# Where two small loads of weights are queued, in a combine of expert outputs that streams 100 MB

## The chip, the cores and the metric

The kernel runs on one core of a Trainium2 chip. Its engines that matter here are VectorE (in the profile DVE), ScalarE (ACT) and SyncE (SP), and the 16 DMA engines that carry data between HBM and the on-chip memory, SBUF. The metric is the time of one execution in microseconds, as the device measures it; of several runs the median counts. The names with a q (SPq, ACTq) are the queues in which an engine's sequencer issues transfers and waits for semaphores.

## The reference

```
weights = combine_weights[..., np.newaxis]
return np.sum(expert_outputs * weights, axis=2).astype(np.float32)
```

`expert_outputs` is 16 x 1024 x 2 x 512 (batch, sequence, k, hidden) and `combine_weights` 16 x 1024 x 2, both float32. For each of the 16,384 tokens the outputs of two experts, rows of 512, are each multiplied by one number and added. 67 MB are read and 33.5 MB are written.

## The kernel before

The tokens are spread over the 128 partitions, 128 for each partition. The first 120 of a partition (`main`) are a contiguous run of HBM, cut into ten tiles of J = 12 tokens; the last 8 (`LAST`) are a second run and make the eleventh tile. The helper `rows` gives, for a token's place and a count, the part of the tensor in one or the other run. A tile `et` holds 12 tokens x 1024 values for every partition, 48 KB of it, and the pool `ipool` has four such buffers. The result is written into the first half of the same buffer (`ot`), so a buffer comes free when its store has landed.

All weights of a partition, 256 numbers, lie in one tile `wt`. Two transfers bring them (L54 to L57): 120 KB for the first 120 tokens (960 bytes for a partition) and 8 KB for the last 8 (64 bytes for a partition). Both are the first instructions in ScalarE's queue. A one-element activation behind them (L60) makes ScalarE load its table early.

The loop (L62) runs over the eleven tiles. SyncE issues the loads (L69): the first tile in two pieces, the first two tokens (1,024 KB, cut into rows of 4 KB) and the other ten (5,120 KB), every other tile in one. The first four tiles need no buffer to come free; the load of tile g from 4 on waits until the store of tile g - 4 has landed. For the first nine tiles VectorE multiplies the whole tile by the weights (L78), adds the halves (L79), and ScalarE issues the store (L80). In the last two tiles ScalarE multiplies the first expert's rows, token by token (L86). VectorE does the rest, for the tenth tile as a whole (L101, L102) and for the last one token by token (L90), and SyncE issues both stores (L103). The scheduler that builds the program keeps the program's order on each engine but for small shifts: it puts the store of the ninth tile (tile 8, counted from 0) between the activations of the tenth.

Each engine issues in its own order, and an instruction that waits holds up everything behind it on that engine. SyncE has the loads and the last two stores, ScalarE the weights, the other stores and its activations. SyncE's transfers are in queue q1 and ScalarE's are in q10.

Of the kernel before, what the change touches and what calls it, by code (L numbers as in the profile page):

```python
# [1 line left out]

# [4 lines left out]


@with_exitstack
def kernel(  # L10
    ctx: ExitStack,
    tc: tile.TileContext,
    expert_outputs: bass.AP,
    combine_weights: bass.AP,
    out: bass.AP,
):

    nc = tc.nc  # L20
    b, s, k, h = expert_outputs.shape
    assert k == 2
    n = b * s
    P = nc.NUM_PARTITIONS
    per = n // P
    assert per * P == n
    J, LAST = 12, 8
    main = per - LAST
    assert main % J == 0
    eo = expert_outputs.rearrange("b s k h -> (b s) (k h)")  # L30
    cw = combine_weights.rearrange("b s k -> (b s) k")
    o = out.rearrange("b s h -> (b s) h")

    def rows(x):

        a = x[0 : P * main, :].rearrange("(p t) f -> p t f", p=P)
        b = x[P * main : n, :].rearrange("(p t) f -> p t f", p=P)
        return lambda t, c: a[:, t : t + c, :] if t < main else b[:, t - main : t - main + c, :]

    eo, cw, o = rows(eo), rows(cw), rows(o)  # L40

    dt = mybir.dt.float32
    mult = mybir.AluOpType.mult
    add = mybir.AluOpType.add
    copy = mybir.ActivationFunctionType.Copy

    last = main // J

    wpool = ctx.enter_context(tc.tile_pool(name="w", bufs=1))
    ipool = ctx.enter_context(tc.tile_pool(name="in", bufs=4))  # L50

    wt = wpool.tile([P, per * k], dt)

    for t, c in ((0, main), (main, LAST)):  # L54
        nc.scalar.dma_start(
            out=wt[:, k * t : k * (t + c)].rearrange("p (t k) -> p t k", k=k), in_=cw(t, c)
        )  # L57

    warm = wpool.tile([P, 1], dt)
    nc.scalar.activation(out=warm, in_=nc.const_aps.tensor(1.0, (P, 1), dt), func=copy)  # L60

    for g in range(last + 1):  # L62
        et = ipool.tile([P, J, k * h], dt)

        ot = et.rearrange("p j f -> p (j f)")[:, 0 : J * h].rearrange("p (j f) -> p j f", f=h)
        t0, c = g * J, J if g < last else LAST

        for a, m in ((0, 2), (2, c - 2)) if g == 0 else ((0, c),):
            nc.sync.dma_start(  # L69
                out=et[:, a : a + m],  # L70
                in_=eo(t0 + a, m),
                max_dma_last_dim=k * h * 4 if g + a == 0 else None,
            )
        if g < last - 1:

            wb = wt[:, g * J * k : (g + 1) * J * k].unsqueeze(2).to_broadcast([P, J * k, h])
            ek = et.rearrange("p j (k h) -> p (j k) h", k=k)
            nc.vector.tensor_tensor(out=ek, in0=ek, in1=wb, op=mult)  # L78
            nc.vector.tensor_tensor(out=ot, in0=et[:, :, 0:h], in1=et[:, :, h : 2 * h], op=add)  # L79
            nc.scalar.dma_start(out=o(t0, c), in_=ot)  # L80
            continue


        for i in range(c):
            t = t0 + i
            nc.scalar.activation(  # L86
                out=et[:, i, 0:h], in_=et[:, i, 0:h], func=copy, scale=wt[:, 2 * t : 2 * t + 1]
            )
            if g == last:
                nc.vector.scalar_tensor_tensor(  # L90
                    out=ot[:, i, :],
                    in0=et[:, i, h : 2 * h],
                    scalar=wt[:, 2 * t + 1 : 2 * t + 2],
                    in1=et[:, i, 0:h],
                    op0=mult,
                    op1=add,
                )
        if g < last:
            w1 = wt.rearrange("p (t k) -> p t k", k=k)[:, t0 : t0 + c, 1:2]
            x1 = et[:, :, h : 2 * h]  # L100
            nc.vector.tensor_tensor(out=x1, in0=x1, in1=w1.to_broadcast([P, c, h]), op=mult)  # L101
            nc.vector.tensor_tensor(out=ot, in0=et[:, :, 0:h], in1=x1, op=add)  # L102
        nc.sync.dma_start(out=o(t0, c), in_=ot[:, 0:c])  # L103


# [1 line left out]
_INS = ['expert_outputs', 'combine_weights']  # L107
_OUTS = [((16, 1024, 512), 'float32')]


# [23 lines left out]
```

## Time and profile before

| | |
|---|---|
| median of 7 runs | 239.09 us (238.93 to 240.9) |
| the profiled execution | 238.93 us, its span 237.2 us |
| DMA | 3728 packets, 100.80 MB, mean 425 GB/s |
| VectorE busy | 193.9 us (82%) |
| ScalarE busy | 14.0 us (6%) |
| the whole-tile multiply, L78 | 9 x 12.96 us |
| the whole-tile add, L79 | 9 x 6.56 us |
| a full tile's load, issue to landing | 29.9 us (median of 9) |
| a store from ScalarE, issue to landing | 32.9 us (median of 9) |
| the weights, issue to landing | 120 KB: 4.2 us; 8 KB: 17.0 us |

The span is the time from the first to the last instruction that the profile shows; the execution's own time is 1.7 us longer. Times of a line are of a profiled execution and are given from the span's start. The time from issue to landing contains what a transfer waits for others in its queue. The share of DMA is the mean over the 16 engines.

### The profile page before, as it was taken

The page shows a single profiled execution, that of the slowest core. Times are in us where ns is not written, and L with a number is a line of the kernel's source. Part 1 is how long each engine was busy: PE and PEld are TensorE (multiplying, and loading weights), DVE is VectorE, ACT ScalarE, POOL GpSimd, SP SyncE. Part 2 cuts the span into 40 slices and gives each one's busy share as a digit, 9 for nine tenths or more (in the row PEclk, how much of TensorE's full clock was granted, in tenths as well). Part 3 has the DMA queues.
Part 4 walks back from the last instruction along what each step waited for, and adds up shares of the span by engine and source line. Part 5 has one row for each costly group of instructions (what it writes and reads, how often), then busy time and mean ns, then how long its engine had stood idle before and what let it go on. Part 6 is the DMA issues. An engine that isn't in the chain of part 4 may idle for free.

```text
span 237.2 us, 154 instructions
## 1 busy us (share of the span) xinstructions
DVE 193.9 (82%) x28; ACT 14.0 (6%) x22; POOL 0.2 (0%) x4
## 2 busy tenths in 40 slices
DVE  0009999999999999999999889969996998785710
ACT  2000000000000000000000000000000000740800
POOL 0000000000000000000000000000000000000000
DMA  8999999979899999999797999999997979999997
GB/s 308 443 465 398 398 431 497 398 332 531 357 439 444 419 464 464 398 398 531 332 531 332 464 410 452 464 464 398 398 522 340 531 332 464 459 403 442 398 442 310
DMA packets 3728, 100.80 MB, mean 425 GB/s; under 512 B 528, under 2 KB 656, under 8 KB 912
## 3 DMA queue, kind: packets, MB, share of 16 engines
q1 hardware_dynamic: 2144, 72.35, 71.1%
q10 hardware_dynamic: 1584, 28.44, 27.9%
HBM read 67.24 MB, written 33.55 MB: 425 GB/s over the span
## 4 chain that ended last, share of the span: by engine, by line
DMA 59%; DVE 33%; ACT 2%; DVEq 0%; ACTq 0%; issue 0%; SPq 0%
DMA et<-in_expert_outputs_dram 30%; DMA out_dram<-et 29%; DVE et L78 22%; DVE et L79 11%; ACT et L86 2%; DVE et L90 1%; DVEq L129 0%; ACTq L129 0%; SPq L69 0%; DVEq L78 0%; ACTq L86 0%
## 5 line engine op out<-in xcount | busy, mean ns | idle before, releaser
L78 DVE TENSOR_TENSOR et<-et,wt 128x12288 f32<-128x12288 f32 x9 | 116.6, 12956 | 25.0 <-DMA et<-in_expert_outputs_dram 25.0
L79 DVE TENSOR_TENSOR et<-et 128x6144 f32<-128x6144 f32 x9 | 59.0, 6558 | 0.3
L86 ACT ACTIVATE et<-et,wt 128x512 f32<-128x512 f32 x20 | 12.5, 711 | 209.1 <-DMA et<-in_expert_outputs_dram 209.1
L90 DVE SCALAR_TENSOR_TENSOR et<-et,wt 128x512 f32<-128x512 f32 x8 | 5.6, 746 | 3.9 <-ACT et L86 3.7
L101 DVE TENSOR_TENSOR et<-et,wt 128x6144 f32<-128x6144 f32 x1 | 6.6, 6557 | 2.3 <-DMA et<-in_expert_outputs_dram 2.3
L102 DVE TENSOR_TENSOR et<-et 128x6144 f32<-128x6144 f32 x1 | 6.6, 6558 | 0.9 <-ACT et L86 0.9
L60 ACT ACT_TABLE_LOAD x1 | 1.3, 1283 | 1.7 <-PEq L118 1.7
L60 ACT ACTIVATE warm<-const-float32-1.0 128x1 f32<-128x1 f32 x1 | 0.2, 203 | 0.0
L118 POOL MEMSET const-bfloat16-1.0<- 128x1 bf16 x1 | 0.1, 103 | 0.0
L118 POOL MEMSET const-uint8-127<- 128x1 uint8 x1 | 0.1, 102 | 0.0
L118 POOL MEMSET const-float32-0.0<- 128x1 f32 x1 | 0.1, 100 | 0.2 <-issue 0.2
L118 POOL MEMSET const-float32-1.0<- 128x1 f32 x1 | 0.1, 99 | 0.0
## 6 DMA issues: line engine op xcount, KB each, us to landing
et<-in_expert_outputs_dram SPq DMA_DIRECT2D x9, 6144.0 KB, 29.9
out_dram<-et ACTq DMA_DIRECT2D x9, 3072.0 KB, 32.9
et<-in_expert_outputs_dram SPq DMA_DIRECT2D x1, 5120.0 KB, 17.0
et<-in_expert_outputs_dram SPq DMA_DIRECT2D x1, 4096.0 KB, 25.1
out_dram<-et SPq DMA_DIRECT2D x1, 3072.0 KB, 14.7
out_dram<-et SPq DMA_DIRECT2D x1, 2048.0 KB, 10.0
et<-in_expert_outputs_dram SPq DMA_DIRECT2D x1, 1024.0 KB, 5.1
wt<-in_combine_weights_dram ACTq DMA_DIRECT2D x1, 120.0 KB, 4.2
```

Of the source, the lines that this page charges most:

```text
L60: nc.scalar.activation(out=warm, in_=nc.const_aps.tensor(1.0, (P, 1), dt), func=copy)
L78: nc.vector.tensor_tensor(out=ek, in0=ek, in1=wb, op=mult)
L79: nc.vector.tensor_tensor(out=ot, in0=et[:, :, 0:h], in1=et[:, :, h : 2 * h], op=add)
L86: nc.scalar.activation(out=et[:, i, 0:h], in_=et[:, i, 0:h], func=copy, scale=wt[:, 2 * t : 2 * t + 1])
L90: nc.vector.scalar_tensor_tensor(out=ot[:, i, :], in0=et[:, i, h : 2 * h], scalar=wt[:, 2 * t + 1 : 2 * t + 2], in1=et[:, i, 0:h], op0=mul ...
L101: nc.vector.tensor_tensor(out=x1, in0=x1, in1=w1.to_broadcast([P, c, h]), op=mult)
L102: nc.vector.tensor_tensor(out=ot, in0=et[:, :, 0:h], in1=x1, op=add)
L118: nc = _bacc.Bacc("TRN2", target_bir_lowering=False, num_devices=1)
```

## The change

Both weight loads are issued by SyncE and not by ScalarE. The first stands behind the load of the first two tokens and ahead of the rest of tile 0; the second, for the last tile's tokens, stands behind the load of the fourth tile. The one-element activation becomes ScalarE's first instruction. The number of buffers gets a name and stays 4. The computation and the sizes of all transfers are unchanged.

```diff
-    J, LAST = 12, 8
+    J, LAST, BUFS = 12, 8, 4
...
-    ipool = ctx.enter_context(tc.tile_pool(name="in", bufs=4))
+    ipool = ctx.enter_context(tc.tile_pool(name="in", bufs=BUFS))
 
     wt = wpool.tile([P, per * k], dt)
 
-    for t, c in ((0, main), (main, LAST)):
-        nc.scalar.dma_start(
+    warm = wpool.tile([P, 1], dt)
+    nc.scalar.activation(out=warm, in_=nc.const_aps.tensor(1.0, (P, 1), dt), func=copy)
+
+    def load_weights(t, c):
+        nc.sync.dma_start(
             out=wt[:, k * t : k * (t + c)].rearrange("p (t k) -> p t k", k=k), in_=cw(t, c)
         )
-
-    warm = wpool.tile([P, 1], dt)
-    nc.scalar.activation(out=warm, in_=nc.const_aps.tensor(1.0, (P, 1), dt), func=copy)
 
     for g in range(last + 1):
...
                 max_dma_last_dim=k * h * 4 if g + a == 0 else None,
             )
+
+            if g + a == 0:
+                load_weights(0, main)
+            elif g == BUFS - 1:
+                load_weights(main, LAST)
         if g < last - 1:
```

## The prediction

> **What bounds the kernel now.** I read the DMA queues first, then the busy time by stages, then the chain that ended last, then SyncE's waits, and last the first 40 us of the timeline and the rows of the weights' tile. The page's part on DMA queues comes first, because reading 67.24 MB and writing 33.55 MB is nearly all that this kernel does:
>
> ```profile
> q1 hardware_dynamic: 2144, 72.35, 71.1%
> q10 hardware_dynamic: 1584, 28.44, 27.9%
> HBM read 67.24 MB, written 33.55 MB: 425 GB/s over the span
> ```
>
> q1 is SyncE's queue and q10 is ScalarE's. Both run on the same 16 DMA engines, and the last column is the time that their packets took as a share of all 16 over the span. 71.1% + 27.9% = 99.0% of 237.2 us is 234.8 us: the packets leave about 2.4 us of the span free. The stages show where that is (per row: length, then busy time of VectorE, ScalarE and GpSimd, the clock, the DMA share, GB/s; a packet is booked where it starts, so a share can pass 1):
>
> ```profile
> 0.00:1.60 1.60, 0.00 (x0) 0.00 (x0) 0.20 (x4) 1.00 0.00 0
> 1.60:4.00 2.40, 0.00 (x0) 1.49 (x2) 0.00 (x0) 1.00 0.91 269
> 4.00:18.40 14.40, 0.03 (x1) 0.00 (x0) 0.00 (x0) 1.00 1.07 456
> 18.40:38.00 19.60, 19.57 (x3) 0.00 (x0) 0.00 (x0) 1.00 1.02 441
> ...
> 60.00:216.00 156.00, 145.94 (x16) 7.47 (x12) 0.00 (x0) 1.00 1.00 432
> 216.00:226.40 10.40, 6.42 (x9) 5.02 (x8) 0.00 (x0) 1.00 1.01 433
> ...
> 236.00:237.20 1.20, 0.00 (x0) 0.00 (x0) 0.00 (x0) 1.00 0.00 0
> ```
>
> Nothing moves for 1.60 us at the front and 1.20 us at the back; between 1.6 and 4 us the engines start up, and from then on they have packets all the time. At 432 GB/s the 2.40 us of start-up would carry 1.04 MB, and at 269 they carried 0.65 MB, so the start-up loses 0.39 MB / 432 GB/s = 0.9 us. That is all that an edit at the front can find. VectorE, busy for 193.9 us, has 43 us of idle time and is not the bound, though the chain that ended last names it:
>
> ```profile
> DMA 59%; DVE 33%; ACT 2%; DVEq 0%; ACTq 0%; issue 0%; SPq 0%
> ```
>
> The chain goes back through VectorE for the tiles that were in SBUF already. The DMA engines are full beside it, so a microsecond saved on VectorE would only move a transfer in a queue that doesn't run dry. What SyncE does meanwhile:
>
> ```profile
> SPq L69 <- DMA out_dram<-et: 173.9, 7, 45.6
> SPq L69 <- DMA et<-in_expert_outputs_dram: 15.0, 1, 15.0
> ```
>
> After its first five loads SyncE waits for stores to land before it may refill a buffer. Its own issuing time is not scarce. The start:
>
> ```profile
> 0.72 0.97 ACTq L55 DMA_DIRECT2D wt<-in_combine_weights_dram  x2
> 0.73 2.52 SPq L69 DMA_DIRECT2D et<-in_expert_outputs_dram  x5
> 1.72 1.28 ACT L60 ACT_TABLE_LOAD   x1 [1.72 <-PEq L118]
> ...
> 18.38 12.96 DVE L78 TENSOR_TENSOR et<-et,wt 128x12288 f32<-128x12288 f32 x1 [18.38 <-DMA et<-in_expert_outputs_dram]
> ...
> 37.96 0.35 ACTq L80 DMA_DIRECT2D out_dram<-et  x1
> ```
>
> The rows of the weights' tile give their issue (ns, shortest, median and longest of the two) and the time from issue to landing:
>
> ```profile
> L55 ACTq DMA_DIRECT2D wt<-in_combine_weights_dram x2: 446/468/491, 0.7 to 1.2; - x2
> ...
> DMA to landing us min/median/max: 4.2/10.6/17.0
> ```
>
> The 8 KB transfer, issued at 1.2, landed 17.0 us later, at about 18.2. So ScalarE's queue is already empty for 20 us when the first store enters it at 37.96. What the change says it brings there is mostly there before.
>
> **The change part by part.** The sum is made against the profiled execution: 238.93 us, of which 237.2 are its span and 1.7 lie around it. The median of the runs shown is 239.09, 0.16 above it.
>
> 1. The two issues leave ScalarE (0.97 us, 0.72 to 1.69). Its table load moves up to about 0.7. ScalarE's next work for a tile is at 202.80, so this is worth 0 by itself. The first load may gain: the chain shows 0.42 us for its issue, with ScalarE issuing beside it, and later issues of the line have a median of 0.328. If that is the neighbour's doing, the first packet comes 0.09 us earlier. Bounds: 0, and a gain of 1.0 us, if the whole start-up loss of 0.9 goes too. I take a gain of 0.1, since the remaining loss is that of a first transfer with nothing before it, which stays.
>
> 2. The weights' packets. In the first 38 us q10 carried only them: 288 packets, 0.13 MB, 1.1% of the 16 engines' time, or 0.42 us. The same packets now go through q1. They are moved and not removed: 0. Between 4 and 18.4 us, where they alternated with the loads, the rate was 456 GB/s, after it 441, with no weights; so the alternation cost nothing that could come back. Bounds: 0.4 either way, their whole time.
>
> 3. The first weight issue on SyncE stands ahead of the 5,120 KB of tile 0. SyncE needs 0.33 to 0.57 us for an issue, ScalarE needed 0.49; the 5,120 KB are issued at 0.73 + 0.42 + 0.49 = 1.64 instead of 1.15. A first packet came 1.60 - 0.73 = 0.9 us after the issue's start, so theirs can come from 2.5. The queue needs them when 1,024 KB and 120 KB are through: 1.6 + 2.7 (1.17 MB at 432) + 0.9 of start-up = 5.2. Cover of 2.7 us, cost 0; bare, it would be 0.49. The first multiply, at 18.38, waits for the 5,120 KB, which lie behind the weights in the same queue: it needs no new wait. Tile 0's own loads move by less than 0.5 us in either direction, and VectorE's 43 us of idle time takes that.
>
> 4. The second weight issue on SyncE, behind tile 3's load. In the built order it waits for the semaphore of the first two tokens, which landed at 0.73 + 5.1 = 5.8; SyncE comes there at 0.73 + 2.52 + 0.49 = 3.7, so it stands for 2 us and issues for 0.45. Behind it is the load of tile 4, issued at 63.99, when the first store has landed (37.96 + 26.0). SyncE's own spare time is 58 us; q1 holds 25 MB, 58 us at 432 GB/s. Cost 0. Its 8 KB land after tile 3's load (issued near 2.9, 69.3 us to landing, so 72); they are first read for the last tile, at 219.76.
>
> 5. ScalarE's queue has its first transfer at 37.96 instead of 0.72, so a queue's first start (0.9 us by the row above) falls on the first store. q1 holds loads until 72, so the engines don't stand. Cost 0; bare, 0.9.
>
> 6. In the built order the store of tile 8 now stands behind 7 and not 8 activations of tile 9. It was issued at 203.10, during the first of them, and lands 24.8 us later, at 228, with 8 us of other stores behind it. At most one activation (0.71) earlier, worth 0.
>
> Sum: 238.93 - 0.1 = 238.8, and with the 0.16 to the median 239.0 us.
>
> A rule against the change, on parts 3 and 4. The rows first: the two issues lasted 0.49 and 0.45 us beside SyncE's five. The Trainium skill, page "DMA: Bandwidth & Descriptors", section "Issuing engines are not separate DMA queues", says that all issuing engines feed the same 16 DMA engines, so that issuing from several at once saves nothing but sequencer time. The trace agrees that the engines are shared (99.0% together). Taken alone, the rule lets this change give back the saved 0.94 us, and the time would be 240.0; by the rows, where SyncE is 2.7 and 58 us ahead, it is 239.0.
>
> **The rivals.**
>
> R1, slower: q1 runs dry at the small transfer. Between 4 and 6 us q1 is now the only queue. If the 120 KB are through before the 5,120 KB are ready, the engines stand for a new start: 0.9 from issue to packet and 0.9 of start-up, +1.8, 240.8 us. It decides from the point where the 5,120 KB come later than 5.2 us. Against it: that needs a 2.7 us delay, and the boundary of 1,024 to 5,120 KB showed none (456 GB/s). The second one, near 72 us, has stores beside it.
>
> R2, slower without a cause in the edit: four of the seven runs lie at 238.93 to 239.09, three at 239.99 to 240.9. Nothing in the profile says what lifts the three. If the changed kernel's median falls among them, it is 240.0 to 240.9, about 240.5.
>
> R3, faster: the start-up loss was two queues starting at once. All of part 1's upper bound comes: 239.09 - 1.0 = 238.1 us. For it: the weights' packets took their places among the first loads'. Against it: the loss is there before the packets can be alternating much, and 0.42 us of them have to be carried somewhere.
>
> **How the numbers follow.** The measurement can tell about 0.5%, or 1.2 us, from no change: under 237.9 is faster, over 240.3 slower. Forecast 0.68, R1 0.08, R2 0.13, R3 0.11. Slower: R1, and 0.08 of R2 (its part above 240.3): 0.16. Faster: 0.05 of R3, which ends just short of the bound, and 0.03 for the kernel before falling among its own higher runs where the two are compared: 0.08. The rest is 0.76. The range goes from R3's 238.1 to R1's 240.8.
>
> **What would show it.** Right: both queues again sum to about 99.0% of the span, q1 with some 0.2% more and q10 less; nothing moves for 1.5 to 1.6 us at the front; the rate from 4 to 18.4 us is as before; SyncE's wait for stores starts later and ends at the same time. Wrong: a stage between 4 and 8 us with a share well under 1 (R1), a first multiply over 0.5 us away from 18.38, or a start-up stage near 430 GB/s (R3). The prediction fails too if the first store, as its queue's first transfer, lowers the rate between 38 and 60 us.

## The result, and the profile after

The changed kernel takes 240.96 us in the median of 23 runs (239.15 to 243.93); the kernel before took 239.10 in 60 runs beside it (238.93 to 240.9). The ratio of the means is 1.0048 [1.0034, 1.0062]; it leaves out four slow runs, at 242.74 to 243.93 and over 1.5% above the fastest, of which nothing on record says what sets them apart, and with them it would be 1.0068. By the ratio that is half a per cent, at the edge of what the forecast called no change; the median lies beyond 240.3, from which the forecast said slower, and 0.16 us above the end of its range. The best run, 239.15, is within 0.3 us of the kernel before; but only 3 of the 23 lie within 0.5 us of it, against 32 of the 60 runs of the kernel before beside them and 100 of its 137 in the sets that follow. The upper runs are not the same either: the 28 of the kernel before lie at 239.85 to 240.9, most of the changed kernel's at 240.4 to 241.4. So it is mostly the typical run that moved.

The profiled execution of the changed kernel is 240.01 us, its span 238.2, 1.08 above the profiled execution before. A second one, taken later, is 240.11. Both lie about 0.9 us below the median: the profile shows part of the loss, and no profile of a typical run at 241 was caught.

The DMA queues of the kernel after (packets, MB, share of the 16 engines' time):

```profile
q1 hardware_dynamic: 2432, 72.48, 71.2%
q10 hardware_dynamic: 1296, 28.31, 27.6%
HBM read 67.24 MB, written 33.55 MB: 423 GB/s over the span
```

The 288 packets of the weights have gone from q10 to q1, as the prediction said. The two shares make 98.8% of 238.2 us, 235.3 us, where it was 234.8: the same bytes took 0.5 us more, and the engines stood for 2.9 us instead of 2.4. The stages of the kernel after show where (length, busy time of VectorE, ScalarE and GpSimd, clock, DMA share, GB/s):

```profile
1.60:4.00 2.40, 0.00 (x0) 0.61 (x2) 0.00 (x0) 1.00 0.85 265
4.00:18.40 14.40, 0.18 (x1) 0.00 (x0) 0.00 (x0) 1.00 1.06 456
...
38.00:60.00 22.00, 21.97 (x3) 0.00 (x0) 0.00 (x0) 1.00 0.98 411
...
76.00:84.00 8.00, 8.00 (x2) 0.00 (x0) 0.00 (x0) 1.00 1.11 443
...
226.40:234.00 7.60, 3.71 (x6) 2.19 (x4) 0.00 (x0) 1.00 0.94 403
226.40:236.00 9.60, 3.71 (x6) 2.19 (x4) 0.00 (x0) 1.00 0.97 418
236.00:237.00 1.00, 0.00 (x0) 0.00 (x0) 0.00 (x0) 1.00 0.24 98
```

and four of the same stages before (the rows from 226.40 overlap):

```profile
76.00:84.00 8.00, 8.00 (x2) 0.00 (x0) 0.00 (x0) 1.00 1.02 442
...
226.40:234.00 7.60, 0.00 (x0) 0.00 (x0) 0.00 (x0) 1.00 1.01 433
226.40:236.00 9.60, 0.00 (x0) 0.00 (x0) 0.00 (x0) 1.00 0.98 418
236.00:237.00 1.00, 0.00 (x0) 0.00 (x0) 0.00 (x0) 1.00 0.00 0
```

Up to 60 us hardly anything is lost: the start-up runs at 265 GB/s where it ran at 269, the rest is as before. Between 76 and 84 us the packets took a share of 1.11 instead of 1.02 for the same rate, (1.11 - 1.02) x 8 = 0.7 us more. The row from 226.4 to 234 has 403 GB/s instead of 433, but a packet is booked where it starts, and the next 2 us make it up: from 226.4 to 236 both kernels move 418 GB/s. In this run, then, the engines don't stand before 236; they end later.

How much later can be read from the packets. Their records don't name the engine, but packets that follow each other without a gap make sixteen chains, one for each engine. Before, all sixteen end between 235.8 and 236.0 us; here fifteen end between 236.2 and 236.7, and one at 237.1. The 0.7 us near 80 us, on all engines, and 0.4 us on this one make up the 1.08 us of this run.

What happens just before 76 us is in the queues' parts from 72.4 to 76.0 us. After:

```profile
q10 hardware_dynamic: 62, 1.52, 98.2%
q1 hardware_dynamic: 63, 0.00, 1.2%
```

Before:

```profile
q1 hardware_dynamic: 32, 1.57, 100.8%
q10 hardware_dynamic: 16, 0.39, 25.3%
```

This is the reading on which the rest hangs. The 8 KB of the last tile's weights are rows of 64 bytes, 128 packets, eight for each engine. They stand in q1 behind tile 3's load, and there they meet the second store in q10. The two queues take turns by packet, not by byte: 63 packets of 64 bytes and 62 packets of a store went through in the same 3.6 us. The store moved 1.52 MB, the loads nothing; before, the loads moved 1.57 MB there and the store 0.39. The Trainium skill, page "DMA: Bandwidth & Descriptors", section "Queues, rings and completion order", says that an engine goes round between the queues it has work for packet by packet; 62 against 63 agrees, where the profile counts each row as a packet.

So the store of tile 1 landed at 77.4 instead of 85.6, and everything behind the small packets in q1 came late. The page's DMA issues of the kernel after (x count, KB each, median us to landing):

```profile
et<-in_expert_outputs_dram SPq DMA_DIRECT2D x9, 6144.0 KB, 38.1
out_dram<-et ACTq DMA_DIRECT2D x9, 3072.0 KB, 28.1
...
out_dram<-et SPq DMA_DIRECT2D x1, 2048.0 KB, 7.3
```

with the small transfer in the list of transfers, and the timeline where VectorE and ScalarE wait for it:

```profile
wt<-in_combine_weights_dram SPq DMA_DIRECT2D x1, 8.0 KB, 71.9
```

```profile
97.72 12.96 DVE L83 TENSOR_TENSOR et<-et,wt 128x12288 f32<-128x12288 f32 x1 [1.56 <-DMA et<-in_expert_outputs_dram]
...
223.58 5.02 ACT L91 ACTIVATE et<-et,wt 128x512 f32<-128x512 f32 x8 [9.47 <-DMA et<-in_expert_outputs_dram]
```

Loads take 38.1 us from issue to landing instead of 29.9, stores 28.1 instead of 32.9. Only part of the loads' 8.2 us is delay: since store 1 lands early, tile 5's load is issued at 77.46 instead of 85.69, and the next one at 103.18 instead of 107.51. Every load from tile 4's on lands 3.8 us later than before, tile 4's at 97.7 instead of 93.9. Tile 4's multiply, which ran at 96.23 without a wait, waits for its load and starts at 97.72. The last load lands at about 223.5 instead of 219.7, the last store is issued at 230.13 instead of 226.32. Beside the last store only store 9 feeds the engines, until 232.6 (before until 231.5), so the stock of other work is 2.5 us where it was 5.2. In this run that was still enough. The chain that ended last has more of the loads now; their share of it was 30% and the stores' 29%:

```profile
DMA et<-in_expert_outputs_dram 37%; DMA out_dram<-et 23%; DVE et L83 22%; DVE et L84 11%; ACT et L91 2%; DVE et L95 1%; DVEq L134 0%; ACTq L134 0%; SPq L69 0%; SPq L58 0%; DVEq L83 0%; ACTq L91 0%
```

### The profile page after: what moved, and what is told of

The parts are those of the page before. It is cut to its first block, busy times and chain, and to the rows that moved or that the text cites. A ratio compares the mean times of both kernels' runs of the same rounds, so it can differ in the third digit from the quotient of the medians.

```text
span 238.2 us, 154 instructions
## 1 busy us (share of the span) xinstructions
DVE 194.1 (81%) x28; ACT 14.0 (6%) x22; POOL 0.2 (0%) x4
## 4 chain that ended last, share of the span: by engine, by line
DMA 60%; DVE 33%; ACT 2%; SPq 0%; DVEq 0%; issue 0%; ACTq 0%
DMA et<-in_expert_outputs_dram 37%; DMA out_dram<-et 23%; DVE et L83 22%; DVE et L84 11%; ACT et L91 2%; DVE et L95 1%; DVEq L134 0%; ACTq L134 0%; SPq L69 0%; SPq L58 0%; DVEq L83 0%; ACTq L91 0%
## 6 DMA issues: line engine op xcount, KB each, us to landing
et<-in_expert_outputs_dram SPq DMA_DIRECT2D x9, 6144.0 KB, 38.1
out_dram<-et ACTq DMA_DIRECT2D x9, 3072.0 KB, 28.1
```

## The experiments

The first theory (T) is this one: the late small packets give the store of tile 1 the loads' turns, the loads run behind from there, and the time is lost in the meeting near 80 us and at the end. Its rivals were: the place of the 120 KB on SyncE, with its slowed packets near 5 us (C); a ScalarE queue that is empty when the first store enters it (E), against a loss that comes wherever the first stores meet running loads (W); the moment at which the first store is issued (B); and chance, the upper runs that the kernel before has too. Unless said, an experiment computes the whole output. "n of m near the best" counts runs within 0.5 us of that kernel's own fastest; in the kernel before it is 73% of the runs in these sets (69 to 83% by set), so a ratio of 1.002 mostly tells how many runs lie about 1 us up.

### One part of the change at a time

The early weights as changed, the late ones back on ScalarE at the start:

```diff
-    def load_weights(t, c):
-        nc.sync.dma_start(
+    def load_weights(t, c, queue=nc.sync):
+        queue.dma_start(
...
                 load_weights(0, main)
-            elif g == BUFS - 1:
-                load_weights(main, LAST)
+                load_weights(main, LAST, nc.scalar)
```

> The 120 KB of weights stay in SyncE's queue behind the first two tokens; the 8 KB go in ScalarE's queue at the start. Theory T (the 64-byte packets of the 8 KB, behind tile 3's load, take turns with the first stores' packets, so the stores run ahead, their queue runs empty, and its restart costs the engines 0.6 us): as before, 239.1 us, one loss of 0.6 us near 41 us and none near 80. Rival Q (the first store suffers as the first transfer of ScalarE's queue): as before too. Rival S (the 120 KB ahead of the 5,120 KB cost the time): as after, 240 to 241 us.

Measured: 239.79 us (239.04 to 240.96, 12 runs), ratio 1.0021 [1.0, 1.0042], 6 of 12 near the best. The opposite, the 120 KB back on ScalarE and the 8 KB as changed:

```diff
-                load_weights(0, main)
+                load_weights(0, main, nc.scalar)
             elif g == BUFS - 1:
                 load_weights(main, LAST)
```

> The 120 KB go in ScalarE's queue at the start; the 8 KB stay in SyncE's queue behind tile 3's load. Theory T: as after, 240 to 241 us, with the 8 KB landing near 77 us, store 1 near 77 instead of 85.6, and tile 4's load some 4 us later than before. Rival Q: as before, 239.1, since ScalarE's queue has been started. Rival S: as before, 239.1.

Measured: 239.79 us (239.13 to 241.03, 12 runs), ratio 1.0026 [1.0004, 1.0048], 5 of 12. The queues behave as T says: store 1 landed at 77.3, tile 4's load at 96.8, loads took 38.1 and stores 27.7 us, as in the kernel after. But the ratio is about half of the change's, and its profiled run (239.13, among its best) shows no extra packet time near 80 us (share 1.00), and the engines don't stand at the end (433 GB/s from 226.4 to 234). In that run the order that T names cost nothing by itself; it opens the way to a loss. And the early part alone, barely resolved, costs about as much, which T can't explain; the two add up to nearly the change's 1.0048, though each interval goes down to nearly 1. The first experiment's profiled run (240.73) shows C's sign: a packet of the 5,120 KB took 0.57 us longer at 5.3 us, and the chain of packets that holds it ends at 237.8, 1.8 us after the other fifteen.

### The late weights elsewhere

Behind tile 1's load, where they come up in q1 at another time (in the second kernel `g == 2`, behind tile 2's):

```diff
-            elif g == BUFS - 1:
+            elif g == 1:
                 load_weights(main, LAST)
```

> As after, but the 8 KB stand behind tile 1's load and not tile 3's, so their packets come near 32 us, before any store is issued (37.8). Theory T: no store can gain turns, 239.1 us, the loads and stores timed as before (store 1 landing near 85.6). Rival Q and rival S: as after, 240 to 241.

> As after, but the 8 KB stand behind tile 2's load, so their packets come near 50 us, in the middle of the first store. Theory T: store 0 lands near 55 us instead of 63.9, the stores' queue is empty until store 1 is issued at 57.3, and a second loss of 0.6 us stands near 60 instead of near 80: 240 to 241 us. Rivals Q and S: as after, 240 to 241, with no sign at 60 us.

Measured: behind tile 1, 240.07 us (239.05 to 240.89, 12 runs), 1.0028 [1.0009, 1.0048], 2 of 12. Its loads and stores take 30.5 and 33.8 us, as before the change, so T's 239.1 missed: without any trading of turns the upper runs are still there. Behind tile 2, 240.50 us (239.14 to 241.19, 12 runs), 1.0031 [1.0006, 1.0057], 4 of 12. Here the small packets did meet the first store, which landed at 56.4 with the 8 KB at 56.5 (T had expected 55), loads take 37.6 us and the last one lands at 224.0; the expected second loss near 60 us wasn't there. Its last store was issued at 230.66, and the engines had nothing for about 0.4 us, in the mean, near 231.

Both loads at the front of q1, behind the 5,120 KB of tile 0, where no store can meet them:

```diff
-            if g + a == 0:
+            if g == 0 and a > 0:
                 load_weights(0, main)
-            elif g == BUFS - 1:
                 load_weights(main, LAST)
```

> As after, but both weight loads stand in SyncE's queue behind the whole of tile 0, so their packets come near 18 us, with no store about and no packet of a tile waiting behind the 4 KB rows of the first two tokens. ScalarE's queue is empty up to the first store, as in after. Theory C, if what hurts near 5.3 us belongs to the start-up: as before, 239.1 us. If it belongs to small packets ahead of large ones: slowed packets near 18.5 us and 239.8. Rival Q (the first store as the first transfer of its queue): 240 to 241.

> The eighth experiment's kernel once more, beside the two others and on the same chip. If its 1.0021 was a real difference: 1.002 again, with most runs above 239.3. If it was chance: 1.000, with two runs in three near 239.1 as in the kernel before.

Measured: 240.02 us (239.06 to 240.84, 12 runs), 1.0021 [1.0002, 1.0041], 3 of 12; and again, 239.23 us (238.97 to 240.83, 12 runs), 1.0016 [0.9993, 1.0039], 7 of 12. By the middles of the intervals more than half of the loss is gone without the meeting near 72 us, but both intervals reach into the change's own, and whether the rest is real in this kernel is not settled. C's slowed packets near 5 us are not in their profiles. They do go with the place of the 120 KB: between 5.1 and 5.7 us single packets of 40 KB took 0.16 to 0.72 us longer than their like in each of the six profiles with the 120 KB ahead of the 5,120 KB in q1, and in none of the other fourteen.

### The small packets added to the kernel before

This leaves the weights as they were before and adds small loads that nothing reads. First two of 8 KB in rows of 64 bytes, eight packets per engine each, behind tiles 3 and 5 on SyncE; then one of 8 KB in 16 rows of 512 bytes, one packet per engine, behind tile 3:

```diff
+        if g in (3, 5):
+            xt = wpool.tile([P, LAST * k], dt, name=f"extra{g}")
+            nc.sync.dma_start(out=xt.rearrange("p (t k) -> p t k", k=k), in_=cw(main, LAST))
```

```diff
+        if g == 3:
+            xt = wpool.tile([16, 128], dt, name="extra")
+            src = combine_weights.rearrange("b s k -> (b s k)")
+            nc.sync.dma_start(out=xt, in_=src[0 : 16 * 128].rearrange("(p f) -> p f", p=16))
```

> The kernel before, its weights in ScalarE's queue as they were, and two more loads of the same 8 KB (128 rows of 64 bytes, into tiles that nothing reads) in SyncE's queue, behind the loads of tiles 3 and 5. Theory C: each hands some 8 turns to the stores and sets the loads back by 3.8 us against them; the last load lands near 227 us instead of 219.7, the last store is issued near 234 instead of 226.3, and the DMA engines stand at the end: 241 to 243 us. Rival S (only the 120 KB ahead of the 5,120 KB cost): 239.1 us.

> The kernel before, and one more load of 8 KB in SyncE's queue behind tile 3's load, as 16 rows of 512 bytes, into a tile that nothing reads: the same bytes as the late weights, but one packet for each DMA engine where those have eight. Theory C (a small packet takes a whole turn from the loads, whatever its size): the loads lose one or two turns, store 1 lands near 84 us and not near 77, no second loss near 80 us; as before, 239.1. If the mere presence of a small transfer in SyncE's queue did it: as in the second experiment, 239.8, ratio 1.0026.

Measured: 241.16 us (239.31 to 242.45, 12 runs), 1.0064 [1.0033, 1.0095], 3 of 12; and 239.14 us (239.08 to 240.61, 12 runs), 0.9999 [0.9983, 1.0014], 11 of 12. The intervals are apart: 8 KB in one packet per engine cost nothing that twelve runs can tell, and two of them in eight packets per engine cost 0.3 to 1%. The pair differs in the number of loads too, though: one load in eight packets is the second experiment, and its interval, from 1.0004, overlaps that of the one packet. The queues of the second from 72.4 to 76.0 us:

```profile
q1 hardware_dynamic: 47, 0.79, 51.4%
q10 hardware_dynamic: 31, 0.76, 49.1%
```

16 of q1's 47 packets are the small ones and 31 are loads; the loads keep moving 0.79 MB. The last load lands at 221.7, so half of the change's delay of the loads is there, at no cost. The stage near 80 us differs accordingly; one small packet per engine, then two loads of eight:

```profile
76.00:84.00 8.00, 8.00 (x2) 0.00 (x0) 0.00 (x0) 1.00 1.02 442
```

```profile
76.00:84.00 8.00, 8.00 (x2) 0.00 (x0) 0.00 (x0) 1.00 1.07 443
```

The size of the delay at the end was overestimated: with two loads the last load landed at 223.0 and the last store was issued at 229.65 in the profiled run, where T had 227 and 234. Loads take 42.4 us and stores 25.6, but the second small load adds little to the first.

The times of all runs together are plainer than the pair. In five kernels a small load of eight packets per engine meets a store: the changed one, the second and fourth experiments, the two added loads, and the changed one with a later store (below). 25 of their 71 runs lie above 240.96 us. None of the other 321 does, 197 of the kernel before and 124 of the other experiments. So the meeting does lift the upper runs.

### Looking again at both kernels

The same kernels once more, for the profile of an upper run:

> The changed kernel once more, for a second trace. Theory C (two costs: single large packets are slowed near 5.3 us right behind the 120 KB in the same queue, so one or two DMA engines fall behind for the rest; and the 8 KB near 77 us give store 1 the turns of tile 4's load): slow first packets of the 5,120 KB again, the spread of one load's sixteen completions over 0.4 us and growing, the last load landing near 223 to 226 us, 240 to 241.5 us. If the cost were in one of the two alone, the sign of the other would be missing.

> The kernel before once more, for a second trace. Theory C: no slowed packet near 5.3 us, store 1 landing near 85.6 us and the last load near 219.7; 239.0 to 239.2 us, or up to 240.5 where a DMA engine falls behind for another reason, near 41 us.

> The kernel with two more loads of 8 KB behind tiles 3 and 5 once more, for a second trace, since its runs went from 239.3 to 242.4 us. Theory C: where it is slow, the sixteen completions of a load are 2 us or more apart, the last load lands near 225, and the DMA engines stand for a while before the last store.

The changed kernel gave 240.11 us. Near 80 us its share is 1.07, so the second loss is there again, while the slowed packets near 5 us, which C rests on, are small (0.16 us); its last load lands at 223.6. One engine ends at 237.2, the others by 236.4; it lost 1.0 us near 81 us. The kernel with two small loads gave 240.88; its last load landed at 223.4 and the last store was issued at 230.0, T's 225 again too late; little stands at its end.

The kernel before gave 239.85, one of its own upper runs. Two stages show it, the end and the stretch from 41.2 to 42.9 us, just after the first store comes in. Its end, and the queue in that stretch:

```profile
236.00:237.00 1.00, 0.00 (x0) 0.00 (x0) 0.00 (x0) 1.00 0.12 49
```

```profile
q10 hardware_dynamic: 3, 0.07, 10.1%
```

In the first profile of this kernel q10 has no packet in that stretch and nothing moves at the end after 236. Here three of the 16 engines took the store's first packet a turn earlier than the others, and the load's packet behind it took about 1.0 us longer on each. At the end three engines stop at 236.7 to 236.9 and the others by 236.3; that these are the same three is likely, but the records don't name them. As far as the packets show, no engine takes over work from another, and all are full, so one that falls behind at 41 us ends late. The time is that of the slowest of the 16, and a mean over them hides it.

### The front of ScalarE's queue

If the empty queue costs something at the first store (E), a queue kept filled should not. The kernel before with two more loads in rows of 64 bytes on ScalarE:

```diff
+    for p in (P, 64):
+        xt = wpool.tile([P, LAST * k], dt, name=f"extra{p}")
+        nc.scalar.dma_start(
+            out=xt[0:p].rearrange("p (t k) -> p t k", k=k), in_=cw(main, LAST)[0:p]
+        )
```

> The kernel before, and behind the weights in ScalarE's queue two more loads of 64-byte rows (128 and 64 rows, into tiles that nothing reads), so that this queue takes turns with the loads until near 43 us and the first store finds it filled: the opposite of what the change aims at. Theory E (the 0.6 us near 41 us, which every trace shows and which makes single DMA engines fall behind, is the price of a queue that starts from empty beside running loads): that loss goes, fewer runs lie near 240, 238.4 to 238.8 us. Rival W (the price is that of the first writes to HBM among reads): the loss moves with the first store to some 44 us, 239.1 to 239.5.

Measured: 240.14 us (239.28 to 240.49, 6 runs), 1.0042 [1.0025, 1.0058], 1 of 6. The queue had packets until 41.8 us, and the loss of about 0.6 us between 41 and 47 us, which the kernel before and after have too, stayed as it was. (It is summed from the packets: there they took 0.6 us per engine longer than elsewhere, where one of 48 KB takes 1.81 us and one of 24 KB 0.91 us.) E falls; W, that the loss comes where a stream of stores first meets running loads, is left, though the loss didn't move to 44 us and the time missed W's too. Yet this kernel has the whole old front, and its 192 small packets more at the start cost nearly as much as the change.

If ScalarE's queue in the first 18 us matters, giving its load back should help. The kernel with both loads behind tile 0, and on ScalarE the two loads of the kernel before, into a tile that nothing reads; then only the 8 KB of them:

```diff
+    xt = wpool.tile([P, per * k], dt, name="extra")
+    for t, c in ((0, main), (main, LAST)):
+        nc.scalar.dma_start(
+            out=xt[:, k * t : k * (t + c)].rearrange("p (t k) -> p t k", k=k), in_=cw(t, c)
+        )
```

> Both weight loads in SyncE's queue behind tile 0, as in the eighth experiment (ratio 1.0021), and the same two loads in ScalarE's queue at the start, as before, into a tile that nothing reads. If traffic in ScalarE's queue during the first 18 us is what the kernel before had ahead of the others: 239.1 us, ratio 1.000. If small loads in SyncE's queue cost: ratio 1.002 again, 239.8 to 240.

> Both weight loads in SyncE's queue behind tile 0, as in the eighth experiment, and one more load of the 8 KB in ScalarE's queue at the start, into a tile that nothing reads. If traffic in ScalarE's queue ahead of the first store keeps DMA engines from falling behind: ratio 1.000 to 1.0005 (0.1 us for the extra packets). If not: 1.002 again.

And the reverse, the 120 KB on ScalarE at the start and the 8 KB on SyncE behind tile 1:

```diff
-                load_weights(0, main)
+                load_weights(0, main, nc.scalar)
-            elif g == BUFS - 1:
+            elif g == 1:
```

> The missing corner of the table: the 120 KB in ScalarE's queue at the start, the 8 KB in SyncE's queue behind tile 1's load, where no store can take their turns. If the 0.2% of the kernels that have the 120 KB in SyncE's queue belongs to the place of the 120 KB: ratio 1.000, 239.1 us. If any small load in SyncE's queue brings it: 1.002, 239.8 to 240.

Measured: with the weights loaded twice, 239.50 us (239.43 to 240.67, 12 runs), 1.0026 [1.0012, 1.004], 8 of 12. Its best runs are 0.4 us above those of the kernel before; that is the 0.42 us of packets which are now moved twice (0.18%), and about 0.08% is left. With the 8 KB alone, 240.13 us (239.05 to 240.44, 10 runs), 1.0026 [1.0006, 1.0047], 1 of 10. The reverse, 240.10 us (239.40 to 240.48, 12 runs), 1.0034 [1.0021, 1.0047], 3 of 12. So neither the place of the 120 KB nor early small packets on ScalarE is the cause alone; of these three only the one with all of the old front's packets comes near the old distribution. The profile of the reverse (240.29 us) shows the same picture as the kernel before in its upper run, in the stretch at 41.2 to 42.9 us and at the end:

```profile
q10 hardware_dynamic: 2, 0.05, 6.7%
```

```profile
236.00:237.00 1.00, 0.00 (x0) 0.00 (x0) 0.00 (x0) 1.00 0.15 66
```

### The moment of the first store

One cause that all these edits could share is a small shift of the first store against the loads' packets (B). It can be moved alone: an addition on VectorE, which nothing reads, between the multiply and the add of tile 0. With 616 numbers the store is issued at 38.76 instead of 37.96, with 1192 at 39.72; and 616 in the kernel after:

```diff
+            if g == 0:
+                xt = wpool.tile([P, 616], dt, name="extra")
+                x = et.rearrange("p j f -> p (j f)")[:, 0:616]
+                nc.vector.tensor_tensor(out=xt, in0=x, in1=x, op=add)
```

> The kernel before, with one more VectorE operation (616 numbers a partition, about 0.80 us, result unread) between the multiply and the add of tile 0, so that the first store is issued 0.8 us later against the loads. Theory B (what counts is where the first store's issue falls against the packet boundaries of the sixteen DMA engines: boundaries come every 1.81 us; in every trace so far they fall 1.1 to 1.7 us behind the issue and the loads lose some 0.6 us; where one falls later than about 1.65, that engine takes the store a turn early and ends 1 us behind the others; where they fell 0.1 to 0.7 us behind the issue, as for the second store of the fourth experiment, hardly anything was lost): boundaries at 0.3 to 0.6, the loss near 41 us mostly gone, no run near 240: 238.5 to 239.0, ratio 0.996 to 0.998. Rival N (the upper runs have nothing to do with the issue's place): 239.1 with a third of the runs near 240, as before.

> The same with 1192 numbers, about 1.40 us, so that the next boundaries fall 1.5 to 1.85 us behind the issue, across the limit. Theory B: several engines on either side, most runs near 240 or above, ratio 1.003 to 1.006. Rival N: 239.1 with a third of the runs near 240.

> The changed kernel with the 0.80 us operation of the sixteenth experiment. Its two encounters, the first store near 41 us and the third near 80, both move to boundaries 0.3 to 0.8 us behind the issue; the late 8 KB still give store 1 the turns of tile 4's load, and the last load still lands near 223. Theory B: 238.6 to 239.3, ratio 0.997 to 1.001, so that the changed order of transfers costs nothing by itself. Theory T (the turns and the shorter stock at the end cost by themselves) and rival N: 240 to 241, ratio 1.003 to 1.005.

Measured: 239.43 us (239.05 to 239.77, 12 runs), 1.0003 [0.9988, 1.0017]; 239.56 us (239.05 to 240.1, 12 runs), 1.0011 [0.9997, 1.0025]; in the kernel after 240.54 us (239.05 to 242.77, 12 runs), 1.0042 [1.0023, 1.0062]. The first removed the runs from 239.8 up (none of 12, where the kernel before beside it had 8 of 29) but brought 6 of 12 at 239.54 to 239.77; the second was expected mostly near 240 or above and had 2 of 12 over 240. The loss at 41 us stayed in the first, about 0.7 us. So the moment shifts the distribution a little, and it isn't what makes the changed kernel slow: with the store later it is as slow as without. That run's profile (240.81 us) is the nearest to a typical one that was caught:

```profile
226.40:234.00 7.60, 4.41 (x7) 3.00 (x5) 0.00 (x0) 1.00 0.93 400
...
236.00:237.00 1.00, 0.00 (x0) 0.00 (x0) 0.00 (x0) 1.00 0.70 295
```

Its last load lands at 224.3 and its last store is issued at 230.94, 0.8 us after that of the changed kernel. Here the engines do stand: from 226.4 to 236 they move 399 GB/s instead of 418, and in the chains of packets eleven of them have nothing for 0.3 to 0.8 us near 231, 0.4 us in the mean of the sixteen. Fourteen end at 236.7 to 236.9 and two at 237.6 and 237.9, when the kernel before has nothing left to do.

## Why the prediction was wrong

**The front was right in the mean.** The start-up stage ran at 265 GB/s (269 before), so part 1's gain of 0.1 and the rival R3's 1.0 us weren't there; the first multiply began at 18.22 instead of 18.38. Part 2: 456 GB/s from 4 to 18.4 us in both. Part 3: the 5,120 KB were issued at 1.73 (1.64 predicted), and there is no gap between 4 and 8 us: R1's dry queue did not come. But single packets there took longer, which no mean shows, and the first experiment leaves the cost of this part open, at 1.0021 [1.0, 1.0042]. Part 5: 411 GB/s from 38 to 60 us in both, so the first store in an empty queue costs nothing more than it did before, and the experiment with the filled queue agrees.

**The failed step is part 4**, "Cost 0. Its 8 KB land after tile 3's load ..., so 72". SyncE did wait and issue as described, at 5.67, and its own time is indeed free. But the 8 KB landed at 77.6 and not at 72: 128 packets of 64 bytes were costed as 8 KB, and each engine's eight of them each cost a whole packet of a store in the other queue. In place of the cost of 0 stood 0.7 us near 80 us in the first profile and (1.07 - 1.02) x 8 = 0.4 in the second. The prediction looked for what the small transfer would wait for, and not for what waits behind it in q1. R1 even named the place, "The second one, near 72 us, has stores beside it", and took it as a protection: the stores do keep the engines busy, but in the turns of the loads, which the last tile needs first.

**The last store was in no part of the sum.** Part 6 looked at the store of tile 8 and rightly gave it 0: it was issued 0.28 us after the first activation of tile 9 began, as before (0.30). But since the loads land 3.8 us later, the last store is issued 3.8 us later too, with 2.5 us of other work beside it and not 5.2. In the two profiles of the changed kernel, where it was issued at 230.1 and 230.2, that covered it; in the two where it came at 230.66 and 230.94 the engines stood for about 0.4 us.

**The sum itself was made over means.** It added shares of 16 engines, and a loss on one to three of them vanishes in such a share: 0.12 in one row of 1 us in the upper run of the kernel before, with 0.92 us on the whole execution.

**The rule that was weighed** gave 240.0, nearer than the forecast, but by a cause that isn't there: SyncE's two issues delayed nothing, as the equal rate from 4 to 18.4 us and the wait until 5.67 show.

**R2 was given too little.** Its words, slower without a cause in the edit, put the chance at 0.13 and the time at 240.0 to 240.9. In fact 20 of 23 runs lie above 239.65, with the median just beyond R2's end. The share of runs near the best goes with the kernel: 73% in the kernel before (53% in the 60 runs beside the change), 92% with one small packet per engine, 8 to 58% where the weights' places were changed and nothing was loaded twice. It isn't fixed in one kernel either: two sets of the same one had 3 and 7 of 12. Still, a spread of four low and three high runs was a sign of something that an edit can move, and it was read as chance.

**What the runs show, and what stays open.** Shown: the trading of turns at 72 us and its delay to the end (profiles of both kernels, of the 120 KB put back, and of the added loads), and that such a meeting costs time, since no run above 240.96 us is without one. That one packet per engine costs nothing is measured, to within 0.14%; that the packets and not the number of loads make the difference is argued from the turns. The size isn't split cleanly: 0.0048 in all, while the edits to the front with no late small load on SyncE beside a store have ratios of 1.0016 to 1.0042, with overlapping intervals. The late load's own share of the change can thus lie anywhere from little to about 0.3%. The other part shows, in the profiles that caught it, as one to three engines that end 0.4 to 2 us after the others. In some they took a turn early at the first store; in the first, third and fourth experiments chains that end late hold the packets slowed near 5 us. The place of the 120 KB, early small packets on ScalarE, an empty queue and the moment of the store were each moved alone, and none accounts for it. Its cause stays open, and so does a typical run of 241, which no profile caught. No kernel of the study was measurably faster than the kernel before.

## What to carry to other kernels

Count a transfer's packets per engine, not its bytes, when another queue is full beside it: each small packet lets a whole large packet of the other queue pass, so small rows belong where no other queue competes, or into one packet per engine. A row of one stage can move a packet's time into the next row, so join the rows before reading that engines stand, and compare landings before calling a longer time from issue a delay. In this kernel, bound by DMA, the time was that of the slowest of the 16 engines, so look at the last stage of the profile and at the spread of runs before costing an edit at nothing. Ask of a moved transfer not only what it waits for, but what waits behind it in its new queue.

## What was unexpected of the hardware

- Two queues shared the engines packet for packet whatever their size: 62 packets with 1.52 MB against 63 with 4 KB, in 3.6 us.
- About 0.6 us is lost from 41 to 47 us, where the first store starts beside running loads, in both kernels and the experiments whose packets were compared there, also when ScalarE's queue still held packets at that time. A second such loss, near 80 us, came only with the late small load in eight packets per engine, and not in all its profiles.
- An engine that fell behind didn't make it up in these traces: in the upper run of the kernel before, three of 16 took the first store's packet early, and 195 us later three ended 0.4 to 1.0 us after the others.
